# Hybrid decoder layer on one core: the FFN's up projection from seven block products for 768 tokens, the down projection as a stage behind it, the output projection by token groups

## The chip, the core and the metric

The kernel runs on one core of a Trainium2 chip. The metric is the device time of one execution in microseconds (us). The core has five engines with one instruction stream each, and each works through its stream in order: TensorE (PE in the profile) multiplies matrices into PSUM, VectorE (DVE), ScalarE (ACT) and GpSimd (POOL) do elementwise work, and SyncE (SP) issues most of the DMAs. Engines wait for one another by semaphores.

## The reference

One layer is computed for a prompt of 1024 tokens and for 8 samples of 8 tokens, with the same weights, all in fp32 (model width 1024, FFN width 3072). The parts that the change touches are the last three lines of the layer:

```python
m = (g[:, :, 0] * (br_lru @ w_br_lru) + g[:, :, 1] * (br_attn @ w_br_attn)
     + g[:, :, 2] * (br_mem @ w_br_mem))
x = x + rms_norm(m @ w_out, g_post_mix)                       # w_out 1024 x 1024
up, ffn_conv_new = causal_dwconv(rms_norm(x, g_pre_ffn) @ w_up, ffn_conv0, w_ffn_conv, b_ffn_conv)
gate, val = jnp.split(up, 2, axis=-1)                         # w_up 1024 x 6144, convolution of width 3
x = x + rms_norm((jax.nn.gelu(gate) * val) @ w_down, g_post_ffn)   # w_down 3072 x 1024
```

Before them stand a norm, the input projection, a recurrent unit, two kinds of attention and three branch projections. They are the same in both kernels.

## The kernel before, in words

Activations lie with the channel on the partitions and the token along the row: a tensor of width 1024 is 8 tiles of 128 partitions by 1088 elements (1024 prompt tokens, then the 64 sample tokens). The 1088 tokens are worked in three groups, `GROUPS`, of 384, 384 and 320.

Every fp32 operand of a product is split in two: a rounded part (`wh`, `hh`, ...: the cast, on ACT) and the rest (`wl`, `hl`, ...: a subtraction, on POOL for weights, on DVE or POOL for activations). `mm3` issues three matmuls for a pair of tiles: high by high, high by low, low by high. One output tile of 128 channels and one token group of a projection with 1024 inputs is thus 8 x 3 = 24 matmuls into one PSUM bank.

Weights come through `Stream` (L202 to L225): a list of tiles in the order of use. `load` issues the DMA into a raw tile `wr`; `split` issues the cast `wh` (ACT, L209) and the subtraction `wl` (POOL, L211) of 128 x 1024 elements; `get` hands out the next pair; `ahead(raw, sp_)` splits the next `sp_` tiles and loads `raw` more. The split of a tile is issued where `ahead` is called, so it stands in ACT's and POOL's streams behind whatever the program issued before.

Work beside the matmuls is written as generators that hang in two lanes. `pump` advances them a step after each PSUM bank, `drain` runs them to their end. The order of instructions is thus fixed by the program (a scheduler moves single instructions by a few places).

The output projection (L1424 to L1452) goes over the 8 output tiles `j`. For the first three, one weight tile serves all three token groups, 72 matmuls in a row; the other five weight tiles are kept (`kept`) and used group by group, so that `post_mix(g)` (L1388) of one group runs beside the products of the next. `evac_o` copies the bank to `ob` (ACT, L1427) and squares it (ACT, L1353; the squares are added up on DVE, L1357). `unit` calls `W.ahead` behind the evacuation of a tile's first group. `post_mix(g)` needs the sum of squares over the channels (matmuls with a column of ones, L833, whose result `norm_bc` spreads by matmuls, L356), scales `ob` (DVE, L1397), adds the residual (POOL, L1398), does the same sums again for the FFN's norm and splits the result into `h2h` and `h2l`.

The FFN goes in six groups of four tiles (`NFG`, `NG`) of the FFN's width. For each tile `j`, `unit` makes the gate tile and the value tile (a weight tile each, all three token groups, 144 matmuls in all) into the padded tiles `up`, and `ffn_tail` does the convolution of width 3 (`conv`, L596: six DVE instructions of 1024 elements and six of 64 for the two tiles, L600 and L602), the gelu (ACT), the product (DVE, L1506) and the split (ACT, POOL). Behind four tiles the down projection of the group follows and is added to `acc` (DVE, L1691); the last down group is done token group by token group, with the final norm and the outputs behind it. `tail_x` (L1590) fetches the residual for that end.

## Time and profile before

| | |
|---|---|
| median of 3 runs | 2702.36 us (2701.34 to 2702.98) |
| the profiled execution | 2699.19 us, span of its trace 2697.4 us |
| PE busy | 2609.9 us, 97% of the span |
| DVE, ACT, POOL busy | 1248.5 us (46%), 990.3 us (37%), 913.8 us (34%) |
| granted clock of TensorE, mean | 0.986 |
| output projection begins | about 1666 us |
| FFN begins | about 1772 us |
| last group of the down projection begins | about 2610 us |

The span is the time from the first to the last instruction of the trace. The matmul records are pipelined: one is listed with 0.33 us, but the next one starts 0.17 us after it, so durations of PE are read from start to start. "L209" is line 209 of the kernel. The granted clock is the share of full speed (2.4 GHz) that the chip gave TensorE; 0.5 is its lower level, 1.2 GHz.

### The profile page before, as it was taken

What the parts mean: (1) busy time and instruction counts of PE and PEld (TensorE: products, weight loads), DVE (VectorE), ACT (ScalarE), POOL (GpSimd) and SP (SyncE); (2) the same over time, 40 slices, a digit from 0 to 9 for tenths busy, and PEclk for the clock granted to TensorE, in tenths of its full rate; (3) what the DMA queues carried; (4) which work ended last, traced back from release to release, by engine and by line L of the source; (5) the groups of instructions that cost most, each with busy time, mean ns of one, the idle gap of its engine ahead of it and who ended that gap; (6) DMA issues with size and microseconds to landing.
All of it is one profiled execution on the core that took longest, in us unless ns stands there. A gap on an engine that the chain in (4) does not pass through costs nothing.

```text
span 2697.4 us, 43018 instructions
## 1 busy us (share of the span) xinstructions
PE 2609.9 (97%) x16884; PEld 2529.4 (94%) x16884; DVE 1248.5 (46%) x2442; ACT 990.3 (37%) x2071; POOL 913.8 (34%) x939
## 2 busy tenths in 40 slices
PE   8999999998999999999999999999999999999987
PEld 7999999998989898999889999989999999999987
DVE  6465520167686766442333213377052433434357
ACT  6556521254545454445420212343321212222233
POOL 4355422343343433211112122344333343333234
PEclk9999999999999999999999999999999999999998
DMA  9311022221221222324855325141212121111133
GB/s 303 118 40 40 24 66 72 65 78 45 76 69 60 71 68 73 115 85 138 274 183 176 126 88 161 32 150 33 57 40 57 32 60 37 42 48 49 40 108 121
DMA packets 293471, 237.32 MB, mean 88 GB/s; under 512 B 16911, under 2 KB 276792, under 8 KB 293268
## 3 DMA queue, kind: packets, MB, share of 16 engines
q1 hardware_dynamic: 286484, 225.91, 27.0%
q10 hardware_dynamic: 6784, 8.65, 0.9%
q8 instruction: 133, 2.18, 0.3%
q14 instruction: 70, 0.57, 0.1%
HBM read 182.11 MB, written 52.40 MB: 87 GB/s over the span
## 4 chain that ended last, share of the span: by engine, by line
PE 84%; DVE 8%; issue 2%; ACT 2%; POOL 2%; DMA 1%; SPq 0%; ACTq 0%; DVEq 0%; POOLq 0%
PE ps L165 24%; PE ps L167 24%; PE ps L166 24%; PE ps L803 1%; DVE y L927 1%; PE ps L804 1%; PE ps L805 1%; PE ps L908 1%; POOL wl L211 1%; PE ps L910 1%; DVE ob L1397 1%; PE ps L885 1%; PE ps L833 1%; ACT e L933 1%; PE ps L1245 0%
## 5 line engine op out<-in xcount | busy, mean ns | idle before, releaser
L211 POOL TENSOR_TENSOR wl<-wr,wh 128x1024 fp32r<-128x1024 f32 x192 | 472.3, 2464 | 734.3 <-ACT wh L209 517.0
L165 PE MATMUL ps<-hh,wh 128*128 128x384 f32 (+1 forms) x1536 | 513.6, 335 | 2.0 <-ACT e L933 1.0
L167 PE MATMUL ps<-hh,wl 128*128 128x384 f32 (+1 forms) x1536 | 504.0, 328 | 4.2 <-POOL wl L211 4.2
L166 PE MATMUL ps<-hl,wh 128*128 128x384 f32 (+1 forms) x1536 | 503.7, 328 | 0.0
L165 PE MATMUL ps<-h2h,wh 128*128 128x384 f32 (+1 forms) x1152 | 376.6, 328 | 3.2 <-ACT h2h L161 3.2
L166 PE MATMUL ps<-h2l,wh 128*128 128x384 f32 (+1 forms) x1152 | 377.1, 328 | 1.5 <-DVE h2l L162 1.5
L167 PE MATMUL ps<-h2h,wl 128*128 128x384 f32 (+1 forms) x1152 | 376.5, 327 | 0.9 <-POOL wl L211 0.9
L165 PEld LDWEIGHTS ps<-hh,wh 128*128 128x128 f32 x1536 | 290.3, 189 | 14.0 <-issue 7.6
L209 ACT CAST wh<-wr 128x1024 fp32r<-128x1024 f32 x199 | 208.0, 1051 | 253.0 <-PE ps L166 74.3
L167 PEld LDWEIGHTS ps<-hh,wl 128*128 128x128 f32 x1536 | 289.8, 189 | 6.2 <-POOL wl L211 4.8
L166 PEld LDWEIGHTS ps<-hl,wh 128*128 128x128 f32 x1536 | 290.4, 189 | 0.8 <-issue 0.2
L165 PE MATMUL ps<-bh,wh 128*128 128x384 f32 (+1 forms) x768 | 251.2, 328 | 0.0
L166 PE MATMUL ps<-bl,wh 128*128 128x384 f32 (+1 forms) x768 | 250.9, 327 | 0.0
L167 PE MATMUL ps<-bh,wl 128*128 128x384 f32 (+1 forms) x768 | 249.7, 327 | 0.0
L165 PEld LDWEIGHTS ps<-h2h,wh 128*128 128x128 f32 x1152 | 217.1, 189 | 3.5 <-ACT h2h L161 3.5
L166 PEld LDWEIGHTS ps<-h2l,wh 128*128 128x128 f32 x1152 | 217.2, 189 | 2.3 <-DVE h2l L162 2.1
L600 DVE TENSOR_SCALAR cv<-up,pf 128x1024 f32<-128x1024 f32 (+2 forms) x52 | 58.4, 1125 | 346.2 <-ACT up L588 155.5
L167 PEld LDWEIGHTS ps<-h2h,wl 128*128 128x128 f32 x1152 | 217.0, 188 | 1.1 <-POOL wl L211 1.1
L588 ACT COPY up<-ps 128x384 f32<-128x384 f32 (+1 forms) x144 | 63.9, 444 | 364.5 <-PE ps L167 357.5
L166 PE MATMUL ps<-ffl,wh 128*128 128x384 f32 (+1 forms) x576 | 189.6, 330 | 0.0
L167 PE MATMUL ps<-ffh,wl 128*128 128x384 f32 (+1 forms) x576 | 189.0, 332 | 0.2 <-POOL wl L211 0.2
L165 PE MATMUL ps<-ffh,wh 128*128 128x384 f32 (+1 forms) x576 | 187.2, 333 | 1.6 <-DVE acc L1691 1.6
(348 smaller groups left out, 5110.1 us busy)
## 6 DMA issues: line engine op xcount, KB each, us to landing
wr<-in_w_in_dram SPq DMA_DIRECT2D x72, 512.0 KB
wr<-in_w_up_dram SPq DMA_DIRECT2D x48, 512.0 KB
wr<-in_w_down_dram SPq DMA_DIRECT2D x32, 512.0 KB
msd<-sig SPq DMA_DIRECT2D x16, 544.0 KB
brl<-brd SPq DMA_DIRECT2D x16, 544.0 KB
mi<-msd SPq DMA_DIRECT2D x16, 544.0 KB
wr<-in_w_mem_kv_dram SPq DMA_DIRECT2D x16, 512.0 KB
pg<-in_cache_k_dram SPq DMA_DIRECT2D x128, 64.0 KB
```

The source lines that it names most:

```text
L165: pe.matmul(ps, lhsT=lh, rhs=rh, start=start, stop=False)
L166: pe.matmul(ps, lhsT=lh, rhs=rl, start=False, stop=False)
L167: last_mm[0] = pe.matmul(ps, lhsT=ll, rhs=rh, start=False, stop=stop)
L209: (dve.tensor_copy if i == 1 else act.copy)(hi, t)
L211: eng.tensor_tensor(lo, t, f(hi), ALU.subtract)
L588: act.copy(pad[:, hist + g0:hist + g0 + n], ps[:, 0:n])
L600: dve.tensor_scalar(out=o, in0=i, scalar1=wcol(0), scalar2=bcol, op0=ALU.mult, op1=ALU.add)
L803: pe.matmul(o, lhsT=xh, rhs=wh[:, k % 4, :], start=(k == 0), stop=False)
L804: pe.matmul(o, lhsT=xh, rhs=wl[:, k % 4, :], start=False, stop=False)
L805: pe.matmul(o, lhsT=xl, rhs=wh[:, k % 4, :], start=False, stop=(k == NC - 1))
L833: pe.matmul(ps[0:m, i:i + 1], lhsT=sq[:, i * 128:i * 128 + m], rhs=ones[:, 0:1], start=True, stop=True)
L885: pe.transpose(ps[:, i, :], in_=e1[:, (c0 + i) * 128:(c0 + i + 1) * 128], identity=ident)
```

## The change

The output projection now has the token group outside: for each of the three groups all 8 weight tiles are loaded, split and used, 24 units of 24 matmuls each (`W.ahead(1, 1)` stands behind the unit's evacuation and its square). Its inputs lie in tiles `mx_`: for the first two groups they are split where branch 2 ends, for the third by a generator `third_m` that runs beside group 1. In `post_mix` the residual's addition moves from POOL to DVE, and the stores of the new residual are issued in one go. For the last group it splits its result for a plain product; for the first two it forms the operands of the block products: with B11, B12 the upper and B21, B22 the lower half of the 1024 channels for tokens 0 to 383 and 384 to 767, the tiles `T1` to `T4` are sums and differences of them, each split.

The up projection of tile `j` takes [gate; value] as the two block rows (128 channels each) and the two halves of the 1024 inputs as the two block columns: A11, A12, A21, A22. The sums S1 to S4 of the weight blocks are made by four DVE instructions of 128 x 512 (L1735 to L1740), and every operand is cast (ACT) and its rest subtracted (POOL) as a tile `wop` of 128 x 2 x 512. Seven products of 12 matmuls of 384 columns replace eight; the results are put together on DVE out of PSUM (seven additions or subtractions of 384 columns per tile, L1813 to L1836, and one copy on ACT). The last 320 tokens are multiplied as before with A11, A12, A21 and A22 (48 matmuls). For the first two tiles these come behind the block products, from raw weights that are loaded again. The convolution's first step moves from DVE to ACT. The product of gelu and value goes to DRAM (`ff_d`); the down projection follows when all 24 tiles are done, in six groups as before, and reads and splits (`ff_prep`: ACT and DVE) a group of four tiles beside the group before it. `tail_x` is called some groups earlier.

```diff
-RO = (2.0, 1.5)
+RO = (3.0, 3.0)
+OW = (1, 1)
...
-        for j in range(g * NFG, (g + 1) * NFG):
-            for s in range(2):
-                add(("u", j, s), cols(w_up, s * 3 * D + j * 128))
...
+    def conv_steps(pad, sv, hist, out, wcol, bcol):
+        for j in range(hist + 1):
+            for o, i in ((out[:, 0:TP], pad[:, j:j + TP]), (s3(out), sv[:, :, j:j + 8])):
+                if j == 0:
+                    act.activation(out=o, in_=i, func=AF.Identity, scale=wcol(0), bias=bcol)
+                else:
+                    dve.scalar_tensor_tensor(out=o, in0=i, scalar=wcol(j), in1=o, op0=ALU.mult, op1=ALU.add)
+            yield
...
     def post_mix(g):
...
-            pool.tensor_tensor(o, o, x[:, 0:gn], ALU.add)
+            dve.tensor_tensor(o, o, x[:, 0:gn], ALU.add)
...
+            for p in range(4):
+                dve.tensor_tensor(b(0, 0, p), b(0, 1, p), b(0, 0, p), ALU.subtract)
+                t = tmp(384)[:, 0:384]
+                dve.tensor_tensor(t, b(1, 1, p), b(0, 0, p), ALU.subtract)
+                osplit("T2", p, t, pool if p % 2 else dve)
...
-    for j in range(NC - KEPT):
-        out_unit(j, (0, 1, 2), W.get(("o", j)))
-        W.ahead(1, OS[j])
-    kept = {}
-    for g in range(3):
-        for j in range(NC - KEPT, NC):
...
+    def prep_op(i):
...
+        if n == "S2":
+            dve.tensor_tensor(s1, vl[:, lo_], vl[:, hi_], ALU.add)
+            dve.tensor_tensor(s2, s1, gt[:, lo_], ALU.subtract)
+        elif n == "S3":
+            dve.tensor_tensor(gt[:, lo_], gt[:, lo_], vl[:, lo_], ALU.subtract)
+        elif n == "S4":
+            dve.tensor_tensor(gt[:, hi_], gt[:, hi_], s2, ALU.subtract)
...
+        w = slot([128, 2, 4, 128], F32R, "wop")
+        split(src, w[:, 0].rearrange("p k m -> p (k m)"), w[:, 1].rearrange("p k m -> p (k m)"), pool)
...
+    for g in range(3):
+        g0, gn = GROUPS[g]
+        if g == 1:
+            lanes[1].append(third_m())
+        if g == 2:
+            drain((1,))
+        for j in range(NC):
+            wh, wl = W.get(("o", g, j))
+            ps = dense_x(lambda k: wh[:, k, :], lambda k: wl[:, k, :], lambda k: mx_[g][k], gn, NC)
+            act.copy(ob(j, g), ps[:, 0:gn])
+            add_sq(("o", g), ps[:, 0:gn], gn)
+            W.ahead(OW[0], OW[1], O_END)
...
+            pump(*RO)
+        mx_[g] = None
+        lanes[0].append(post_mix(g))
...
+    for i, (j, n) in enumerate(items):
+        if n == "A11g" and j == 0:
+            drain()
...
+        prep_op(i)
+        w = wops.pop(i)
+        if n == "A11":
+            ps = piece(w, op_rhs("B11"), 384, None, True, True)
+            s["p1"] = tmp(384)[:, 0:384]
+            act.copy(s["p1"], ps[:, 0:384])
+        elif n == "A12":
+            ps = piece(w, op_rhs("B21"), 384, None, True, True)
+            dve.tensor_tensor(gates2(s)[0][:, 2:2 + 384], s["p1"], ps[:, 0:384], ALU.add)
+        elif n == "S2":
+            ps = piece(w, op_rhs("T2"), 384, None, True, True)
+            s["u2"] = s.pop("p1")
+            dve.tensor_tensor(s["u2"], s["u2"], ps[:, 0:384], ALU.add)
...
+        prep_op(i + OPA)
...
     for fg in range(NG):
...
+        if fg + 1 < NG:
+            lanes[1].append(ff_prep(fg + 1))
...
-            for g in range(TG, 3):
-                side.append(tail_x(g))
...
+            if fg == NG - 3:
+                for g in range(TG, 3):
+                    side.append(tail_x(g))
```

The stream of ACT in the output projection, before. `ps` is a PSUM bank of one output tile and one token group, `wh` the next weight tile's high part; each line of `ps` belongs to 24 matmuls. Here the second output tile is evacuated, group by group:

```order
L1427 COPY ob2809_17813<-ps2828_17916 128x384
L1353 ACTIVATE t2829_17942<-ps2828_17916 128x384
L209 CAST wh2834_18003<-wr2827_17914 128x1024
L1427 COPY ob2809_17813<-ps2830_17945 128x384
L1353 ACTIVATE t2831_17971<-ps2830_17945 128x384
L209 CAST wh2837_18009<-wr2836_18007 128x1024
L1427 COPY ob2809_17813<-ps2832_17974 128x320
L1353 ACTIVATE t2833_18000<-ps2832_17974 128x320
L1427 COPY ob2810_17814<-ps2840_18015 128x384
L1353 ACTIVATE t2841_18041<-ps2840_18015 128x384
```

And the stream of ACT in the output projection now, in its first token group:

```order
L1760 COPY ob2808_17830<-ps2816_17862 128x384
L1406 ACTIVATE t2817_17888<-ps2816_17862 128x384
L216 CAST wh2818_17890<-wr2800_17751 128x1024
L1760 COPY ob2809_17831<-ps2821_17896 128x384
L1406 ACTIVATE t2822_17922<-ps2821_17896 128x384
L216 CAST wh2823_17925<-wr2820_17894 128x1024
L1760 COPY ob2810_17832<-ps2826_17932 128x384
L1406 ACTIVATE t2827_17958<-ps2826_17932 128x384
L216 CAST wh2828_17961<-wr2825_17929 128x1024
```

Before, the cast of the next weight tile stands behind the first of the three banks that use the present tile, with two banks more to come. Now a tile serves one bank, and the cast of the next tile stands behind that bank's copy and square.

The stream of POOL in the up projection, before. `wl` is a weight tile's rest, `ffl` the rest of an FFN tile; `sp`, `fo` and `up` are small pieces of the convolution's state:

```order
L211 TENSOR_TENSOR wl_19480<-wr_19361,wh_19479 128x1024
L1499 COPY fo_19365<-up_19323 128x2
L1500 COPY fo_19365<-sp_19324 128x16
L162 TENSOR_TENSOR ffl_19496<-cv_19485,ffh_19495 128x1088
L1540 MEMSET up_19552 128x2
L1540 MEMSET up_19556 128x2
L211 TENSOR_TENSOR wl_19587<-wr_19363,wh_19586 128x1024
L1499 COPY fo_19365<-up_19327 128x2
L1500 COPY fo_19365<-sp_19328 128x16
L162 TENSOR_TENSOR ffl_19639<-cv_19628,ffh_19638 128x1088
L211 TENSOR_TENSOR wl_19696<-wr_19483,wh_19695 128x1024
L1499 COPY fo_19365<-up_19552 128x2
```

And the stream of POOL in the up projection now, a little over one tile `j`:

```order
L169 TENSOR_TENSOR wop_21823<-wr_21570,wop_21823 128x512
L169 TENSOR_TENSOR wop_21828<-ws_21739,wop_21828 128x512
L1582 MEMSET up_21880 128x2
L1565 COPY fo_21952<-up_21775 128x2
L1566 COPY fo_21952<-sp_21776 128x16
L169 TENSOR_TENSOR wop_21862<-wr_21572,wop_21862 128x512
L169 TENSOR_TENSOR wop_21887<-wr_21570,wop_21887 128x512
L169 TENSOR_TENSOR wop_21905<-wr_21802,wop_21905 128x512
L169 TENSOR_TENSOR wop_21942<-wr_21802,wop_21942 128x512
L1565 COPY fo_21952<-up_21880 128x2
L1566 COPY fo_21952<-sp_21881 128x16
L1582 MEMSET up_22007 128x2
```

Where two subtractions of 1024 elements for the weights and one of 1088 for the result stood per tile, there are eight of 512 for the weight operands; the result's subtraction has gone from this stream (it is DVE's, in the down stage).

## Rows read from the trace of the kernel before

**Rows 1.** Page, section 4: engines' shares of the chain that ended last.
```profile
PE 84%; DVE 8%; issue 2%; ACT 2%; POOL 2%; DMA 1%; SPq 0%; ACTq 0%; DVEq 0%; POOLq 0%
```

**Rows 2.** Busy by stage: stretch, length, PE, PEld, DVE, ACT, POOL, clock, DMA share, GB/s.
```profile
1666.00:1772.00 106.00, 100.19 (x602) 99.56 (x600) 41.62 (x62) 37.65 (x75) 39.58 (x25) 0.97 0.23 63
1772.00:1847.00 75.00, 69.41 (x394) 66.53 (x394) 51.85 (x83) 32.60 (x66) 34.65 (x44) 0.93 0.43 136
1847.00:2610.00 763.00, 762.80 (x4659) 759.80 (x4659) 293.57 (x408) 191.68 (x328) 271.13 (x259) 1.00 0.15 45
2610.00:2697.00 87.00, 65.38 (x401) 62.91 (x399) 61.62 (x90) 31.64 (x56) 37.17 (x23) 0.86 0.44 152
```

**Rows 3.** Timeline of PE, 320 columns: start us, us, instruction.
```profile
1638.67 0.31 PE L167 MATMUL ps<-bh,wl 128*128 128x320 f32 x1
...
1641.75 0.31 PE L167 MATMUL ps<-bh,wl 128*128 128x320 f32 x1
```

**Rows 4.** Timeline of PE, 384 columns, full clock.
```profile
1643.83 0.33 PE L167 MATMUL ps<-bh,wl 128*128 128x384 f32 x1
...
1646.95 0.33 PE L167 MATMUL ps<-bh,wl 128*128 128x384 f32 x1
```

**Rows 5.** Timeline of a hand-off from PE to ACT.
```profile
1709.60 0.33 PE L167 MATMUL ps<-bh,wl 128*128 128x384 f32 x1
...
1710.03 0.48 ACT L1427 COPY ob<-ps 128x384 f32<-128x384 f32 x1 [3.28 <-PE ps L167]
...
1710.40 0.50 ACT L1353 ACTIVATE t<-ps 128x384 f32<-128x384 f32 x1
```

**Rows 6.** Lines by form, 1560 to 2697 us: busy us, mean ns | idle before, releaser.
```profile
L211 POOL TENSOR_TENSOR wl<-wr,wh 128x1024 fp32r<-128x1024 f32 x96 | 235.7, 2463 | 234.9 <-ACT wh L209 143.7 <-PE ps L166 46.8 <-issue 29.8
...
L602 DVE SCALAR_TENSOR_TENSOR cv<-up,pf,cv 128x1024 f32<-128x1024 f32 x92 | 119.3, 1297 | 0.0
...
L209 ACT CAST wh<-wr 128x1024 fp32r<-128x1024 f32 x95 | 99.2, 1051 | 142.2 <-PE ps L167 62.6 <-PE ps L166 60.0 <-DMA wr<-in_w_down_dram 13.3
...
L1691 DVE TENSOR_TENSOR acc<-acc,ps 128x384 f32<-128x384 f32 x80 | 43.4, 551 | 108.4 <-PE ps L167 108.4
...
L602 DVE SCALAR_TENSOR_TENSOR cv<-sp,pf,cv 128x64 f32<-128x64 f32 x96 | 33.4, 349 | 0.0
L1357 DVE TENSOR_TENSOR t<-t,t 128x384 f32<-128x384 f32 x42 | 32.4, 778 | 48.0 <-ACT t L1353 47.0
L1506 DVE TENSOR_TENSOR cv<-cv,cv 128x1088 f32<-128x1088 f32 x23 | 29.7, 1293 | 4.0 <-ACT cv L1503 2.1
...
L1397 DVE SCALAR_TENSOR_TENSOR ob<-ob,pv,t 128x384 f32<-128x384 f32 x16 | 16.3, 1085 | 4.3 <-ACT t L1367 4.3
...
L162 POOL TENSOR_TENSOR ffl<-cv,ffh 128x384 fp32r<-128x384 f32 x1 | 1.1, 1137 | 0.5 <-ACT ffh L161 0.5
```

**Rows 7.** PE waits by releaser, 1666 to 1772 us: total us, times, longest.
```profile
PE ps L833 <- DVE t L1357: 4.4, 1, 4.4
```

**Rows 8.** Two 10 us windows behind two waits; columns as in rows 2.
```profile
1750.00:1760.00 10.00, 8.55 (x50) 8.50 (x50) 5.86 (x13) 3.19 (x7) 2.15 (x2) 0.74 0.12 35
1780.00:1790.00 10.00, 10.00 (x39) 9.66 (x39) 4.09 (x11) 4.99 (x8) 8.13 (x12) 0.54 0.57 168
```

**Rows 9.** Timeline of DVE and POOL in the FFN stage.
```profile
1957.33 0.84 DVE L600 TENSOR_SCALAR cv<-up,pf 128x1024 f32<-128x1024 f32 x1 [10.73 <-issue]
...
1957.42 0.20 POOL L1500 COPY fo<-sp 128x16 f32<-128x16 f32 x1
...
1962.69 1.21 POOL L1541 COPY sp<-fs 128x16 f32<-128x16 f32 x1 [5.07 <-DVE cv L602]
...
1969.27 2.39 POOL L211 TENSOR_TENSOR wl<-wr,wh 128x1024 fp32r<-128x1024 f32 x1
1969.34 2.93 DVE L600 TENSOR_SCALAR cv<-up,pf 128x1024 f32<-128x1024 f32 x1 [3.98 <-POOL ffl L162]
```

**Rows 10.** PE waits by releaser, 2610 to 2697 us.
```profile
PE ps L1584 <- DMA xl<-x2d: 7.2, 1, 7.2
```

More of the change, by code (lines that the diff above doesn't have):

```diff
@@ L219, in get, with ahead @@
             return self.hl.pop(i)
-        def ahead(self, raw=2, sp_=1):
-            for j in range(sp_):
+        def ahead(self, raw=2, sp_=1, end=None):
+            n = raw + sp_ if end is None else max(0, min(raw + sp_, end - self.i))
+            for j in range(min(sp_, n)):
                 self.split(self.i + j)
-            for j in range(sp_, sp_ + raw):
+            for j in range(sp_, n):
                 self.load(self.i + j)
@@ L1330, in layer_step, with split_m @@
     KEEP = 5
+    G0, G1, G2 = (slice(g0, g0 + gn) for g0, gn in GROUPS)
+    mx_ = [[None] * NC for _ in range(3)]
+    def split_m(j, s):
+        for g in range(2):
+            x = slot((128, T), F32R, "mx")
+            mx_[g][j] = (x[:, G0], x[:, G1])
+            g0, gn = GROUPS[g]
+            split(s[:, g0:g0 + gn], *mx_[g][j])
     def final_m(j, s):
@@ L1340, in final_m, with third_m, ob @@
                 t = slot(name="ml")
-                load(t, ms2[i])
-                mh[i], ml[i] = split_tile(t)
+                load(t[:, 0:768], ms2[i][:, 0:768])
+                split_m(i, t)
+    def third_m():
+        parts = []
+        for i in range(6):
+            x = slot((128, T), F32R, "m2")
+            parts += [x[:, 320 * q:320 * q + 320] for q in range(3)]
+            while len(parts) >= 2 and parts:
+                j = next(j for j in range(NC + 1) if j == NC or mx_[2][j] is None)
+                if j == NC:
+                    break
+                t = tmp(320)
+                load(t[:, 0:320], ms2[j][:, G2])
+                mx_[2][j] = (parts.pop(0), parts.pop(0))
+                yield False
+                split(t[:, 0:320], *mx_[2][j], pool)
+                yield False
     branch(2, load_br(1), RH, final_m)
     x2_d = [dpool.tile([128, T], F32, name=f"x2d{c}") for c in range(NC)]
-    ob = [slot(name="ob") for _ in range(NC)]
+    ob01 = [slot(name="ob") for _ in range(NC)]
+    ob2 = []
+    def ob(j, g):
+        if g < 2:
+            return ob01[j][:, GROUPS[g][0]:GROUPS[g][0] + GROUPS[g][1]]
+        if not ob2:
+            for _ in range(3):
+                x = slot(name="ob2")
+                ob2.extend(x[:, 320 * q:320 * q + 320] for q in range(3))
+        return ob2[j]
     ssq = {}
@@ L1357, in add_sq, with norm_bc @@
             dve.tensor_tensor(ssq[key][:, 0:gn], ssq[key][:, 0:gn], sq[:, 0:gn], ALU.add)
-    def norm_bc(key, gn):
-        for _ in range(dict(x=NYX, f=NYF).get(key[0], NY1)):
+    def norm_bc(key, gn, first=None):
+        for i in range(dict(x=NYX, f=NYF, o=NYO).get(key[0], NY1)):
             yield False
+            if i == 0 and first:
+                first()
         rr = rstd_of(subln_sums(ssq.pop(key), gn), gn, D)
@@ L1416, in post_mix @@
-        for j in range(NC):
-            if g < 2 and j >= HOLD:
-                held[g].append(lambda j=j: h2(j))
-                continue
-            h2(j)
+            o = ob(j, g)
+            h = o
+            dve.scalar_tensor_tensor(out=h, in0=o, scalar=P("g_pre_ffn", j), in1=rb2[:, 0:gn],
+                                     op0=ALU.mult, op1=ALU.mult)
+            p = j % 4
+            if g == 2:
+                hi = opslot("B21" if j >= 4 else "B11", p)[:, G2]
+                lo = opslot("T2" if j >= 4 else "T1", p)[:, G2]
+                h2x[j] = (hi, lo)
+                split(h, hi, lo)
+            elif g == 0:
+                osplit("B21" if j >= 4 else "B11", p, h)
@@ L1450, in layer_step, with dense_x @@
+    def dense_x(wh, wl, xs, gn, nk, ps=None, first=True, last=True):
+        ps = ps or bank()
+        for k in range(nk):
+            mm3(ps[:, 0:gn], wh(k), wl(k), *xs(k), first and k == 0, last and k == nk - 1)
+        return ps
     sfc = a["state_ffn_conv"].rearrange("o b j d -> (o b j) d")
@@ L1461, in load_fs, with put_fo @@
+    def put_fo(j, fo):
+        ft = tmp(256)
+        ps = bank()
         for s in range(2):
[L1462 removed]
+            pe.transpose(ps[0:18, s * 128:(s + 1) * 128], in_=fo[:, s, :], identity=ident)
+        act.copy(ft[0:18, 0:256], ps[0:18, 0:256])
         def put():
[L1465 to L1468 removed]
@@ new lines, in layer_step, with piece, op_rhs, rhs @@
+    blk = {}
+    def piece(w, rhs, gn, ps, first, last):
+        return dense_x(lambda k: w[:, 0, k, :], lambda k: w[:, 1, k, :], rhs, gn, 4, ps, first, last)
+    def op_rhs(name):
+        def rhs(k):
+            x = opt[name, k]
+            return x[:, G0], x[:, G1]
+        return rhs
+    def g2_rhs(half):
+        return lambda k: h2x[4 * half + k]
+    for j in range(NP1):
+        fsput.pop(j)()
+    def gates2(s):
+        s["pg"] = s.get("pg") or pads_of(s["j"], 0)
+        return s["pg"]
```

325 lines of the change are left out of this document (196 added, 129 removed).

## The prediction, made before the changed kernel was run

> **What bounds the kernel now.** I read the chain of waits first: 84% of it is PE, no other engine has more than 8% [rows 1]. A change is worth what it takes from PE, unless something else becomes late. Then busy time by stage, since an average hides the stages the change touches [rows 2]. The reader is to see three things in these rows. In the FFN's long stretch PE is busy 762.80 of 763 us at full clock: there every matmul counts, and DVE (293.57) and POOL (271.13) have room, 74% together. In the output projection PE is idle for 5.8 of 106 us, in the first 75 us of the FFN for 5.6, with the clock at 0.97 and 0.93. In the last down group it is idle for 21.6 of 87.
>
> **The matmuls that go.** A 384-column matmul takes 18 steps in 3.12 us, 0.1733 us each [rows 4]; a 320-column one 21 steps in 3.08 us, 0.1467 [rows 3]. Per FFN tile the first 768 tokens need 7 x 12 = 84 matmuls instead of 96; the last 320 tokens keep 48. So 24 x 12 = 288 matmuls go: 288 x 0.1733 = **-50 us**. Nothing else of PE's work changes in size.
>
> **The output projection, first token group.** The change puts the cast of the next weight tile behind the copy and the square of the present bank on ACT, and only one bank of 24 matmuls uses a tile. That makes a ring. From the start of a bank's last matmul to the copy 0.43 us, to the square 0.37 more [rows 5]; to the cast as much again as between copy and square (0.37, my estimate from the same rows), then the cast 1.05 and POOL's subtraction 2.46 [rows 6]. The third matmul of the next bank needs that result; 21 more follow it, 3.64 us. One turn is 0.43 + 0.37 + 0.37 + 1.05 + 2.46 + 3.64 = 8.3 us for 24 x 0.1733 = 4.16 us of matmuls. Nothing stands in the lanes there yet, so no work covers it: 7 x 4.1 = **+29 us**. Before, two more banks (some 7.7 us) ran behind the cast, which hid all of it. The raw weights are not late: SyncE has little in line there and the DMA share of the stage is 0.23 [rows 2].
>
> **Groups two and three.** The same ring runs with `post_mix` in it. Its steps stand on ACT ahead of casts, and its column sums (six matmuls that wait for DVE) stand on PE between banks. In the order I find five places where PE must wait for more than the ring: three casts behind a run of squares, and two sums that wait for the whole DVE chain of a group. That chain has grown by the additions taken from POOL: 8 scalings at 1.09 us, 8 additions and 7 sums at about 0.78 each [rows 6] are 20 us. These durations were taken beside POOL's subtractions, so that is its long form. It is queued in front of the next bank's sum of squares, and PE's next sum waits for that. The trace of before has this wait once, 4.4 us [rows 7], with two thirds of the chain. Against four banks of 4.16 us that run meanwhile, a chain of 20 us is late by 3 us at least, and by 12 where the additions start late. Nearest to the row of 4.4 is the low end, but there the additions were POOL's; I take 8.4 us for each of the five, **+42 us** (30 to 60).
>
> **The junction.** The old excess goes: 106 us for 384 x 0.1733 + 192 x 0.1467 = 94.7 us of matmuls, 11.3; then 5.6 idle and 7% of 69.4 us of clock, 4.9, together 10.5 [rows 2]. Call it **-22**. In its place come the start of the block products, whose weights stand in POOL's queue behind the subtractions for the operands, some 8 us, and the gates of the first two tiles, which need all of `post_mix` of the third group (16 us by the chain above, with 320 columns, less the block products in front). I take **+23 us** (12 to 30). The two cancel.
>
> **The up stage.** PE needs 84 x 0.1733 + 48 x 0.1467 = 21.6 us per tile, before 23.7. What is new is the load on DVE and POOL. DVE and POOL exclude one another on some instructions [rows 9]: a DVE TENSOR_SCALAR of 1024 elements takes 0.84 us with POOL at rest and 2.93 us when POOL's 2.39 us subtraction has begun 0.07 us before it; a POOL copy of 16 elements takes 0.20 us at 1957 and 1.21 us at 1962, while DVE is in its convolution. So instructions with two SBUF inputs on DVE and all of POOL's add up. Per tile: DVE 4 x 1.30 + 4 x 0.35 + 1.29 for the convolution and the product, and 4 x 0.64 for the weight sums (0.64 for 512 elements is my estimate from 1.29 for 1088 [rows 6]), 10.4 us. POOL 8 subtractions of 512 at 1.40 (between 1.14 at 384 and 2.46 at 1024 [rows 6]), 11.2 us, and six small pieces at 0.2, 1.2 us. Together 22.8 us, over PE's 21.6. DVE has seven more additions out of PSUM, 0.55 each [rows 6], 3.9 us, whose source is not SBUF; if they too find POOL shut out or stand between POOL's work, the sum is 26.7. So a tile costs PE's time and 0.3 us (part of the durations above already holds some waiting) to 5.1 us more. I take 2.0, as a sum of 22.8 leaves no room for two in-order queues that also wait for PE: 22 tiles x 2.0 = **+44 us** (7 to 112). ACT takes the convolution's first step and is far from full: 191.68 of 763 us in the old stage [rows 2].
>
> **The clock.** Behind the 4.4 us wait the next 10 us have a granted clock of 0.74, behind another wait of the junction 0.54 [rows 8]: 2.2 us (26% of 8.55) to 4.6 us lost, at the lower level of 1.2 GHz for part of the time. Before there are three such waits. Now PE waits for about 4 us seven times in the first group, and some seven times for longer. If each cost 2.2 us it would be 31; short waits may cost nothing. I take **+25 us** (0 to 50).
>
> **The rest.** The residual for the end is fetched earlier, so the 7.2 us wait for it [rows 10] goes with some clock behind it: **-10**, and what is late next there is the norm, which is as before. The down stage has its 24 weight splits and additions unchanged; `ff_prep` adds 4 casts and 4 DVE subtractions per 46 us of matmuls. The 24 results pass through DRAM, 0.56 MB each way, in a stage with a DMA share of 0.15 [rows 2], hidden by the matmuls. The first of the six groups has to wait for the last tile's tail: **+5** (0 to 8). Stores of the residual in `post_mix` now go in one piece through SyncE's queue ahead of weight loads; 8 stores of 0.2 MB are covered by the bank in work, and if not it is in the 60 above.
>
> **Sum.** -50 + 29 + 42 - 22 + 23 + 44 + 25 - 10 + 5 = +86 us on the profiled execution of 2699.2 us, 2785. The median is 3.2 us above that execution, so 2788 us.
>
> **Rivals.**
> Output projection late, up stage bound by PE. For it: DVE and POOL are never full in the old stage, and the additions out of PSUM need no port. Against it: 22.8 is more than 21.6 without them. With 7 for the up stage, 35 for groups two and three and 15 for the clock: -50 + 29 + 35 - 22 + 23 + 7 + 15 - 10 + 5 = +32, 2735 us.
>
> Every burst starts slow. If the clock falls in each wait of the output projection, each of 23 banks runs at the lower level from its third matmul on: 21 x 0.1733 = 3.64 us more, 84 us instead of 25, 2847 us. For it: 0.54 in rows 8. Against it: 0.74 in the same rows, and waits of about 4 us as in rows 7. The Trainium skill, "TensorE: Matmul & The Clock Gate", section "HAM oscillation — how this bites in real kernels", tells of a kernel whose short bursts of matmuls between waits each start at the lower clock, and speaks against a loop of this form; by that rule the sum would be this rival's. No run here has a row of such bursts yet. The same time comes if DVE and POOL work fully one after the other: 22 x 5.1 = 112 instead of 44, 2856 us.
>
> Not slower. The ring does not close: casts and subtractions come in time for groups two and three, because `post_mix` in between gives ACT and POOL time to run ahead. Then those groups keep 12 us of waits, the junction 12, the clock loses nothing, the up stage 7: -50 + 29 + 12 - 22 + 12 + 7 - 10 = -22, 2680 us. It decides if the waits outside the first group stay under 34 us together. Against it: the cast stands behind the bank's evacuation in all three groups.
>
> That the change does not do what it says is no rival: PE's listed instructions have the 288 matmuls less, and nothing makes up for them there.
>
> **How the numbers follow.** Forecast 0.52 (2750 to 2825), output projection only 0.21, slow bursts or ports in full 0.15, not slower 0.12. A difference under 0.2% (5.4 us) can't be told from no change; of the last case's 0.12 a quarter falls there. So faster 0.09, same 0.03, slower 0.88. The range leaves out the fast case and the upper end of the slow one: 2708 to 2862 us.
>
> **What the profile after will show.** In the first group of the output projection, PE in bursts of 24 matmuls every 8 us with waits for `wl` of about 4 us; the stage with 60 to 95 us more than before. In the up stage, PE waits for `wop` from POOL, tiles of 23 to 25 us, with DVE and POOL together near 100%. The clock in the output projection near 0.8. The last down group without the wait of 7.2 us. I am wrong if a unit of the output projection takes under 5 us, or if the up stage runs at 21.9 us per tile with PE never waiting; then the second or the last case holds.

## The result, and the profile after

The changed kernel takes 2761.39 us (median of 4 runs, 2760.86 to 2765.28), the kernel before 2702.67 us in the same series: +58.7 us, ratio 1.0219, interval 1.0202 to 1.0237. It is slower, as forecast, inside the range and 27 us under the predicted time. Its profiled execution took 2765.28 us, 66.1 us more than that of before. Of these, 5.2 us lie ahead of the output projection, where the two kernels are nearly the same (it begins at 1665.6 us before and at 1670.8 us now). I count them as scatter between executions: in the runs below, which have the changed kernel's code there, it begins between 1665.3 and 1671.3 us. 61 us are the change's.

The chain of waits has moved away from PE, five points against [rows 1]:

```profile
PE 79%; DVE 7%; issue 5%; POOL 3%; ACT 3%; DMA 2%; SPq 0%; ACTq 0%; DVEq 0%; POOLq 0%
```

Busy time by stage of the changed kernel, in the columns of [rows 2]: first token group of the output projection, the other two, the start of the up stage, the up stage, the down stage, the end.

```profile
1671.00:1750.00 79.00, 51.65 (x193) 46.26 (x193) 5.82 (x11) 14.88 (x25) 16.73 (x8) 0.76 0.31 87
1750.00:1883.00 133.00, 84.80 (x428) 80.70 (x428) 65.56 (x113) 51.01 (x101) 64.58 (x37) 0.76 0.35 102
1883.00:1960.00 77.00, 60.26 (x345) 57.11 (x343) 57.37 (x81) 33.16 (x69) 53.03 (x52) 0.89 0.35 103
1960.00:2426.00 466.00, 466.00 (x2843) 458.16 (x2841) 370.85 (x425) 218.12 (x424) 303.03 (x336) 1.00 0.24 75
2426.00:2704.00 278.00, 278.00 (x1699) 277.71 (x1698) 114.09 (x164) 80.90 (x119) 72.89 (x36) 1.00 0.35 117
2704.00:2763.00 59.00, 43.93 (x266) 41.52 (x264) 42.84 (x75) 16.86 (x30) 25.04 (x18) 0.86 0.37 126
```

The reader should see two halves. In the up and the down stage, 744 us, PE is never idle and the clock is 1.00. Ahead of that, in 289 us, PE is idle for 92 us and runs at 0.76 to 0.89; the same stretch of before had 11 us of idle time in 181 [rows 2]. Who is waited for there:

```profile
PE ps L848 <- DVE t L1410: 31.4, 3, 14.1
PE ps L174 <- POOL wl L218: 26.8, 13, 5.9
PE ps L172 <- ACT wh L216: 24.8, 12, 4.1
...
PE ps L174 <- POOL wop L169: 1.4, 2, 1.0
```

The first row is the column sums that wait for DVE, the next two are the weights of the output projection. The weights of the up stage (`wop`), from which I had expected 44 us, are the last row shown, 1.4 us.

To split the 61 us I take each stage's time from its first matmul to the next stage's first, less 0.1733 us for each of its 384-column and 0.1467 for each of its 320-column matmuls. What is left is waits, lower clock, small matmuls and steps of PE that are a little longer than these:

| us beyond the matmuls | before | now |
|---|---|---|
| output projection, token groups 1 / 2 / 3 | 12.2 together | 45.5 / 33.5 / 37.8 |
| start of the FFN | 15.8 | 24.7 |
| steady FFN; now up 15.0 and down 6.5 | 11.1 | 21.5 |
| last down group | 35.9 | 22.8 |
| sum | 75.0 | 185.8 |

185.8 - 75.0 - 49.9 (the 288 matmuls) = +60.9 us.

One turn of the first token group, in a timeline of the changed kernel: the last matmul of a unit, copy, square and cast on ACT, the next unit's first matmul, the subtraction on POOL, and the first matmul that needs it.

```profile
1706.31 0.34 PE L174 MATMUL ps<-mx,wl 128*128 128x384 f32 x1
1706.69 0.48 ACT L1760 COPY ob<-ps 128x384 f32<-128x384 f32 x1 [8.18 <-PE ps L174]
1707.06 0.50 ACT L1406 ACTIVATE t<-ps 128x384 f32<-128x384 f32 x1
1707.44 1.05 ACT L216 CAST wh<-wr 128x1024 fp32r<-128x1024 f32 x1
...
1708.54 0.52 PE L172 MATMUL ps<-mx,wh 128*128 128x384 f32 x1 [1.89 <-ACT wh L216]
1708.57 2.35 POOL L218 TENSOR_TENSOR wl<-wr,wh 128x1024 fp32r<-128x1024 f32 x1 [7.64 <-ACT wh L216]
...
1710.97 0.69 PE L174 MATMUL ps<-mx,wl 128*128 128x384 f32 x1 [1.58 <-POOL wl L218]
```

From 1706.31 to 1710.97 are 4.66 us. The prediction's sum for this piece was 0.43 + 0.37 + 0.37 + 1.05 + 2.46 = 4.68. The rest of the turn is longer than forecast: the seven turns take 10.35 us on average ((1749.6 - 1677.1) / 7), not 8.3, and the matmul at 1710.97 is listed with 0.69 us where [rows 4] has 0.33.

### The profile page after: what moved, and what is told of

Same layout as the page of the kernel before. It is cut to its first block, busy times and chain, and to the rows that moved or that the text cites. A ratio compares the mean times of both kernels' runs of the same rounds, so it can differ in the third digit from the quotient of the medians.

```text
span 2763.3 us, 43739 instructions
## 1 busy us (share of the span) xinstructions
PE 2599.4 (94%) x16596; PEld 2504.4 (91%) x16596; DVE 1461.9 (53%) x2677; ACT 1113.3 (40%) x2323; POOL 1065.6 (39%) x1074
## 4 chain that ended last, share of the span: by engine, by line
PE 79%; DVE 7%; issue 5%; POOL 3%; ACT 3%; DMA 2%; SPq 0%; ACTq 0%; DVEq 0%; POOLq 0%
PE ps L172 23%; PE ps L174 23%; PE ps L173 22%; POOL wl L218 2%; DVE y L942 1%; PE ps L818 1%; PE ps L819 1%; PE ps L820 1%; PE ps L923 1%; PE ps L900 1%; PE ps L925 1%; ACT e L948 1%; DVE e L956 1%; POOL wop L169 0%; PE ps L1260 0%
## 5 line engine op out<-in xcount | busy, mean ns | idle before, releaser
L218 POOL TENSOR_TENSOR wl<-wr,wh 128x1024 fp32r<-128x1024 f32 x160 | 391.0, 2447 | 878.5 <-ACT wh L216 672.1
L172 PE MATMUL ps<-bop,wop 128*128 128x384 f32 (+1 forms) x1056 | 349.1, 331 | 1.6 <-ACT bop L168 1.6
L173 PE MATMUL ps<-bop,wop 128*128 128x384 f32 (+1 forms) x1056 | 345.0, 327 | 2.2 <-DVE bop L169 2.2
L174 PE MATMUL ps<-bop,wop 128*128 128x384 f32 (+1 forms) x1056 | 344.6, 327 | 2.2 <-POOL wop L169 1.4
L172 PEld LDWEIGHTS ps<-hh,wh 128*128 128x128 f32 x1536 | 290.0, 189 | 14.2 <-issue 7.6
L169 POOL TENSOR_TENSOR wop<-wr,wop 128x512 fp32r<-128x512 f32 x150 | 242.3, 1630 | 36.0 <-ACT wop L168 35.0
L216 ACT CAST wh<-wr 128x1024 fp32r<-128x1024 f32 x167 | 173.7, 1049 | 131.0 <-DMA msd<-sig 68.4
L744 DVE TENSOR_TENSOR sig<-sig,ps 128x384 f32<-128x384 f32 (+1 forms) x72 | 38.3, 531 | 312.0 <-PE ps L174 312.0
L174 PEld LDWEIGHTS ps<-bop,wop 128*128 128x128 f32 x1056 | 199.0, 188 | 3.3 <-POOL wop L169 1.9
L172 PEld LDWEIGHTS ps<-bop,wop 128*128 128x128 f32 x1056 | 199.1, 189 | 2.8 <-ACT bop L168 1.8
L173 PEld LDWEIGHTS ps<-bop,wop 128*128 128x128 f32 x1056 | 199.1, 189 | 2.6 <-DVE bop L169 2.6
L172 PE MATMUL ps<-bh,wh 128*128 128x384 f32 (+1 forms) x576 | 188.6, 327 | 0.0
L173 PE MATMUL ps<-bl,wh 128*128 128x384 f32 (+1 forms) x576 | 188.3, 327 | 0.0
L174 PE MATMUL ps<-bh,wl 128*128 128x384 f32 (+1 forms) x576 | 188.1, 327 | 0.0
```

Source lines behind the costliest of these rows:

```text
L169: (on_lo or dve).tensor_tensor(lo, src, f(hi), ALU.subtract)
L172: pe.matmul(ps, lhsT=lh, rhs=rh, start=start, stop=False)
L173: pe.matmul(ps, lhsT=lh, rhs=rl, start=False, stop=False)
L174: last_mm[0] = pe.matmul(ps, lhsT=ll, rhs=rh, start=False, stop=stop)
L216: (dve.tensor_copy if i == 1 else act.copy)(hi, t)
L218: eng.tensor_tensor(lo, t, f(hi), ALU.subtract)
```

## Experiments

**The cast ahead of the matmuls.** In the output projection's loop:

```diff
             wh, wl = W.get(("o", g, j))
+            W.ahead(OW[0], OW[1], O_END)
             ps = dense_x(...)
             act.copy(ob(j, g), ps[:, 0:gn])
             add_sq(("o", g), ps[:, 0:gn], gn)
-            W.ahead(OW[0], OW[1], O_END)
```

> Changed kernel, with one edit: in the output projection the next weight tile's cast and subtraction are issued ahead of the present unit's matmuls, not behind its evacuation. Ring theory (the wait is the serial chain copy, square, cast, subtraction): the 7 turns of the first token group fall from 10.35 us to about 4.2 us each, -43 us, and the weight waits of groups two and three (some 27 us) mostly go, the DVE waits at the column sums (32 us) stay: about 2695 us. Rival, the raw weight loads or POOL's queue are late too: each unit then takes as long as a load or the 2.5 us subtraction with its hand-offs allows, 6 to 8 us, and the time falls by 20 to 30 us only: about 2735 us.

Measured: 2713.82 us, 47.6 under the changed kernel (ratio to before 1.0041, 1.0027 to 1.0055). By stage (first group; second and third), and PE's waits up to the steady up stage:

```profile
1669.00:1706.00 37.00, 35.02 (x198) 33.71 (x197) 7.17 (x10) 13.52 (x23) 19.14 (x8) 1.00 0.64 180
1706.00:1829.50 123.50, 80.13 (x425) 76.27 (x425) 64.96 (x111) 50.31 (x99) 61.45 (x36) 0.77 0.38 112
```

```profile
PE ps L848 <- DVE t L1410: 30.4, 3, 13.0
PE ps L174 <- POOL wl L218: 13.8, 5, 5.8
PE ps L172 <- ACT wh L216: 7.6, 3, 3.4
```

The ring is open: the first group takes 36.3 us, not 78.8, 3.1 beyond its matmuls, at full clock, and raw loads don't hold it. But the other half of the expectation failed: groups two and three keep 62.0 of their 71.3 us. The sums still wait 30 us, and eight waits for weights stay, 21.4 us together. One tile of lead was enough in the first group and not in the two where `post_mix` shares ACT and POOL.

**Filler in the ring.** In seven units of the first group, matmuls whose result is not used, where PE waits:

```diff
+            if g == 0 and j:
+                last_fill = filler(last_mm[0])            # 12 matmuls of 384 columns ahead of the unit
...
+                    second = pe.matmul(ps[:, 0:gn], lhsT=wh[:, k, :], rhs=rl, start=False, stop=False)
+                    if k == 0:
+                        last_fill = filler(second)        # 12 more ahead of the first with wl
```

> Changed kernel, with 24 matmuls of 384 columns added in each of the last seven units of the first token group, whose result nobody uses: 12 stand where PE waits for the high part of the weights, 12 where it waits for the low part, 2.1 us each in gaps of 2.2 us. Clock theory: of the 10.35 us of a turn, 8.3 are the chain and 2.05 the lower clock behind the waits; with PE kept busy the clock stays up and a turn takes 8.3 us: about -14 us, 2747 us, with a granted clock near 1.0 in that stretch. Rival, the turn is long for another reason (a longer hand-off, late loads): no gain, 2761 us, or up to +7 us where the filler delays the unit.

Measured: 2751.20 us, 10.2 less. The first group, in the changed kernel and here:

```profile
1671.00:1739.00 68.00, 44.99 (x168) 40.23 (x167) 5.08 (x10) 12.11 (x21) 14.08 (x6) 0.75 0.32 90
```

```profile
1671.00:1733.00 62.00, 61.25 (x347) 59.22 (x345) 3.35 (x6) 13.37 (x23) 16.75 (x7) 1.00 0.39 109
```

PE does 168 matmuls more and the stretch ends earlier: it is busy for 61.25 of 62 us and the clock is 1.00 where it was 0.75. The whole group takes 65.7 us, not 78.8, and a turn 8.5 us (five turns from 1681.09 to 1723.51), where the prediction's sum was 8.3. So some 1.9 us of each turn of 10.35 were the lower clock. It is a diagnosis and no remedy, since the waits stay.

**More work for POOL in the up stage.** Two of the eight subtractions per tile are done twice:

```diff
+        if j >= NP1 and n in ("A11", "S1"):
+            pool.tensor_tensor(w[:, 1]..., src, f(w[:, 0]...), ALU.subtract)
```

> Changed kernel, with two of the eight POOL subtractions of 512 elements per FFN tile done twice for 22 tiles (POOL +2.6 us per tile). Shared-port theory: DVE's instructions with two SBUF inputs and POOL's work add up to some 21 of the 21.85 us of a tile already (the union of both in the trace is 96%), so 2.6 us more make a tile 1.0 to 1.8 us longer: +20 to +40 us, 2781 to 2801 us, with PE waiting for the weight operands. Rival, each engine has its own room (POOL at 62 to 72%): no change, 2761 us.

Measured: 2772.64 us, +11.2, between the two. The up stage itself grew by 5.4 us (451.1 us of matmuls at 21.6 are 20.9 tiles), its start by 4.5. A stretch of 300 us in the changed kernel and here:

```profile
2100.00:2400.00 300.00, 300.00 (x1830) 294.65 (x1830) 229.12 (x269) 139.60 (x271) 185.75 (x215) 1.00 0.24 76
```

```profile
2100.00:2400.00 300.00, 300.00 (x1829) 294.93 (x1828) 242.80 (x271) 140.07 (x265) 232.98 (x242) 1.00 0.23 74
```

POOL is busy 47 us more and PE still for 300 of 300, with the same number of matmuls. Nearly all of the growth is at the start: the first four tiles with double work take 25.6, 23.5, 24.5 and 24.1 us, and from the sixth on a tile takes 22.3 to 22.4 us as in the changed kernel. Here are the first 51 us; the changed kernel has 314 matmuls there and no idle time:

```profile
1949.00:2000.00 51.00, 47.93 (x286) 45.67 (x285) 42.80 (x43) 21.87 (x41) 39.80 (x40) 1.00 0.24 65
```

So in the settled stage two more subtractions cost nothing. The union of both engines' busy times, from which I had read a full path, includes their waiting for each other, so it says nothing about room.

Then all eight, with the same line and without its condition on `n`:

> Changed kernel, with all eight POOL subtractions of 512 elements per FFN tile done twice for 22 tiles (POOL +10.3 us per tile, to some 21.5 of its own 21.85). Two more per tile cost the up stage only 5 us, so an instruction can't hold the other engine out for all of its time. Short-hold theory: each holds the shared way for its elements only (some 1.1 of POOL's 1.29 us, 1.1 of DVE's 1.27, 0.07 of its 0.27): 16.8 us per tile in the changed kernel, 19.0 with two more, 25.5 here, so a tile takes 3 to 4.5 us longer: +65 to +100 us, about 2840 us. Rival, no exclusion that counts: POOL is just full by itself, 0 to +20 us, 2761 to 2781 us.

Measured: 2903.99 us, +142.6, more than either theory: the up stage takes 123.6 us more, 5.9 per tile, and a settled tile 28.4 us where it took 22.3. The same stretch, and what PE waits for in it:

```profile
2100.00:2400.00 300.00, 252.30 (x1429) 241.28 (x1429) 227.08 (x209) 106.76 (x209) 275.08 (x254) 0.95 0.18 58
```

```profile
PE ps L172 <- ACT wop L168: 42.9, 19, 4.7
```

PE is busy for 252 of 300 us. It waits for ACT's casts, and ACT in turn stands idle for 56.6 us behind DVE's convolution before it casts the weight sums. The rival falls: POOL's sixteen subtractions at about 1.3 us and its small pieces would fit a tile, but their means here are 1.36 to 1.74 us (one of four rows is shown), and DVE is stretched too. DVE's lines, changed kernel first, then this one with a row of POOL:

```profile
L616 DVE SCALAR_TENSOR_TENSOR cv<-up,pf,cv 128x1024 f32<-128x1024 f32 x53 | 67.6, 1276 | 25.7 <-ACT cv L614 25.7
...
L1826 DVE TENSOR_TENSOR up<-t,ps 128x384 f32<-128x384 f32 x14 | 7.8, 555 | 21.4 <-PE ps L174 21.4
```

```profile
L616 DVE SCALAR_TENSOR_TENSOR cv<-up,pf,cv 128x1024 f32<-128x1024 f32 x42 | 73.2, 1760 | 0.0
...
L1829 DVE TENSOR_TENSOR up<-t,ps 128x384 f32<-128x384 f32 x11 | 6.1, 555 | 17.0 <-PE ps L174 17.0
...
L169 POOL TENSOR_TENSOR wop<-wr,wop 128x512 fp32r<-128x512 f32 x65 | 109.3, 1687 | 0.0
```

The step with two operands in SBUF goes from 1.28 to 1.76 us, the addition out of PSUM stays at 0.555. The Trainium skill, "GPSIMD Engine Reference", section "Key points", has GpSimd share its SBUF interfaces with VectorE, with contention for DVE's instructions with two SBUF inputs; the two rows of each DVE pair agree.

How full was the path in the changed kernel? For three forms the trace gives the shortest, median and longest ns in that stretch:

```profile
L616 DVE SCALAR_TENSOR_TENSOR cv<-up,pf,cv x53: 1270/1273/1287, 2105.8 to 2396.0; 128x1024 f32<-128x1024 f32 x53
L616 DVE SCALAR_TENSOR_TENSOR cv<-sp,pf,cv x53: 270/1315/1337, 2108.7 to 2398.9; 128x64 f32<-128x64 f32 x53
...
L169 POOL TENSOR_TENSOR wop<-wr,wop x81: 1276/1302/2249, 2099.0 to 2398.4; 128x512 fp32r<-128x512 f32 x81
```

The second row shows how much of a duration can be waiting: the step of 64 elements takes 0.27 us at its shortest and 1.3 us in the median. At their shortest, DVE's instructions with two SBUF inputs need 4 x 1.27 + 4 x 0.27 + 1.29 [rows 6] + 4 x 0.68 (the weight sums) = 10.2 us per tile, POOL 8 x 1.28 and some 1.4 for its small pieces, 11.6: together 21.8 us, 24.3 with two more subtractions, 32.0 with eight. The settled tiles took 22.3, 22.3 and 28.4 us. So these times don't all lie one behind the other: some 2 us overlap with two more, at least 3.6 with eight. That is an estimate from three kernels. The edge lies between two and eight more subtractions per tile.

**The residual's addition back on POOL.**

```diff
-            dve.tensor_tensor(o, o, x[:, 0:gn], ALU.add)
+            pool.tensor_tensor(o, o, x[:, 0:gn], ALU.add)
```

> Changed kernel, with the residual's addition behind the output projection put back on POOL as in the kernel before. If the length of DVE's chain is what PE's column sums wait for (32 us in four waits), taking 8 x 0.55 us from DVE per group shortens each wait by 3 to 4 us: -8 to -12 us, about 2751 us. Rival, the square and sum behind each addition then wait for POOL, whose addition takes 1.3 us and stands behind the 2.5 us weight subtractions: no gain or longer, 2761 to 2780 us.

Measured: 2766.02 us, +4.6: the rival, by little. PE's waits:

```profile
PE ps L174 <- POOL wl L218: 29.8, 14, 5.8
PE ps L848 <- DVE t L1410: 27.5, 3, 11.6
```

The sums wait 4 us less (27.5), the weights' rests 3 us more (29.8). Moving the addition to DVE was not what made the change slow.

**Where sums and casts stand.** Three variants of the kernel with the cast first. Two tiles split ahead of use:

```diff
-OW = (1, 1)
+OW = (1, 2)
```

> Changed kernel with the cast ahead of the matmuls (the kernel of 2713.8 us), and the split one tile further ahead: two tiles are split ahead of use, not one. Theory, the weight waits left in groups two and three (3.4 + 5.5 us and 3.7 + 6.3 us, with smaller ones some 22 us) come from casts and subtractions that stand behind the norm's work on ACT and POOL: one unit more of lead takes most of them away, -10 to -20 us, 2694 to 2704 us. Rival, the waits for DVE's chain at the column sums (10.2 and 13.3 us) only grow by what is saved ahead of them: 0 to -8 us, about 2710 us.

Measured: 2705.67 us, -8.1 (ratio 1.0015, 1.0005 to 1.0024), at the border of the two. Then the sums later, with one tile ahead as in the first experiment:

```diff
-NYX = 3
+NYX = 11
-RO = (3.0, 3.0)
+RO = (4.0, 3.0)
```

> The kernel of 2713.8 us, with the steps beside the matmuls taken four per unit, not three, and eight more empty steps ahead of the second column sum of each group, so that DVE's chain starts some 0.7 unit earlier and PE meets the sum about 1.1 units later. Theory, the waits of 10.2 and 13.3 us at the sums come from where the sum stands in PE's stream: they shrink by 5 to 7 us each, with some clock behind them -12 to -20 us, 2694 to 2702 us. Rival, what follows the sum (operands of the block products) is then late by as much: no gain, 2710 to 2720 us.

Measured: 2713.52 us, no gain: the rival. Its waits:

```profile
PE ps L848 <- DVE t L1410: 14.2, 2, 7.7
...
PE ps L174 <- POOL wl L218: 9.3, 6, 3.8
```

The sums' waits halve, from 30.4 to 14.2, and others take their place: the third group has 16.1 us beyond its matmuls where it had 32.2, the start of the up stage 42.4 where it had 26.3. From the end of the second group to the steady up stage it is 139.6 us without the edit and 139.7 with it. Third, one FFN tile more whose 320-token part comes late:

```diff
-NP1 = 2
+NP1 = 3
```

> The kernel of 2713.8 us, with three FFN tiles, not two, whose 320-token part is put behind their block products (14.6 us more of matmuls ahead of the wait for the third group's norm). Theory, the junction's 16 us of waits (7.8 at the column sum, 2.2, 1.3, 2.0, 2.7 around it) are DVE's chain of the third group: they go but for the hand-offs, -8 to -14 us, about 2702 us. Rival, DVE and POOL are shared with the operands and the weights of the block products, so the chain is late by as much again: 0 to -4 us, about 2711 us.

Measured: 2716.14 us, +2.3: the rival, and a little worse. The wait at the third group's sum is 8.8 us, before 7.5.

**Both edits, and the chain made shorter.** The two edits to `OW` and to `NYX` and `RO` together:

> The two edits to the out-projection loop joined: split two tiles ahead (2705.7 us) and the sums later in PE's stream with four steps per unit (2713.5 us). Chain theory: from the last product of the second token group to the steady up stage the time was 138 to 140 us in every variant, wherever single waits stood, because the block products need the finished norm of both groups and its operands, and only 28.5 us of other matmuls lie beside that; so no gain over the first of the two, 2702 to 2710 us. Rival, the waits are a matter of where sums and casts stand: each edit takes its own, 2690 to 2697 us.

Measured: 2705.00 us (ratio 1.0009, 1.0000 to 1.0019), -0.7 against the first of them alone, which is no gain: the kernel before itself moved by 1.5 us between the two series. So far it is the chain theory. The second token group became 8.8 us shorter, and the stretch from its end to the steady up stage 8.6 us longer. And the chain itself, in the kernel with two tiles ahead, leaving out the residual:

```diff
-            dve.tensor_tensor(o, o, x[:, 0:gn], ALU.add)
```

> The kernel of 2705.7 us, leaving out the residual's addition ahead of the FFN's norm (8 DVE additions per token group; the FFN then sees the normed projection alone). Chain theory: each group's chain of DVE work, ACT squares and sums is 8 x 0.55 us shorter, and PE waits for the end of it in each group: -9 to -14 us, 2692 to 2697 us. Rival, the additions are hidden beside the squares or the waits come from the weights' casts: 0 to -3 us, 2703 to 2706 us.

Measured: 2694.76 us (ratio 0.9966, 0.9953 to 0.9978), -10.9. PE's waits with the residual, and then without:

```profile
PE ps L848 <- DVE t L1410: 33.2, 4, 14.6
PE ps L174 <- POOL wop L169: 11.2, 4, 8.6
PE ps L174 <- POOL wl L218: 6.7, 3, 5.0
```

```profile
PE ps L848 <- DVE t L1410: 18.8, 4, 8.1
PE ps L174 <- POOL wop L169: 11.1, 4, 8.9
PE ps L174 <- POOL wl L218: 7.1, 3, 5.3
```

The waits at the sums fall by 14.4 us, of the others only one changes by much (that for `wop` from ACT, 0.5 to 4.4). So the length of `post_mix`'s chain counts in PE's time here. One limit: with the addition goes also DVE's wait for the residual's load, which the timeline of the changed kernel shows inside that chain. Here is the end of the first group's chain in it:

```profile
1770.55 1.48 DVE L1463 TENSOR_TENSOR ob<-ob,t 128x384 f32<-128x384 f32 x3
...
1771.39 0.34 PE L174 MATMUL ps<-mx,wl 128*128 128x384 f32 x1
...
1774.10 1.03 DVE L1463 TENSOR_TENSOR ob<-ob,t 128x384 f32<-128x384 f32 x2 [0.67 <-DMA t<-xsd]
...
1775.96 0.56 DVE L1463 TENSOR_TENSOR ob<-ob,t 128x384 f32<-128x384 f32 x1 [0.82 <-DMA t<-xsd]
...
1776.44 2.15 DVE L1410 TENSOR_TENSOR t<-t,t 128x384 f32<-128x384 f32 x4
...
1778.50 1.68 DVE L1463 TENSOR_TENSOR ob<-ob,t 128x384 f32<-128x384 f32 x2
...
1780.31 1.69 DVE L1410 TENSOR_TENSOR t<-t,t 128x384 f32<-128x384 f32 x3
...
1781.58 1.44 PE L848 MATMUL ps<-ones,t 128*128 128x1 f32 x6 [9.85 <-DVE t L1410]
```

DVE's additions stop twice behind a load, at 1774.10 and at 1775.96; PE has begun its last matmul of a unit at 1771.39 and stands until the sum at 1781.58. In the kernel with two tiles ahead DVE stands idle for such loads for 1.6 us in all. But no run takes the loads away alone, so how the 10.9 us divide between the additions and the loads stays open.

**Other work ahead.** The kernel with two tiles ahead, with the products of the first token group first and four weight operands ahead:

```diff
-OPA = 2
+OPA = 4
-    items = [(j, n) for j in range(NP1) for n in SEVEN] + \
+    items = [(j, n) for j in range(NP1) for n in SEVEN[:2]] + \
+        [(j, n) for j in range(NP1) for n in SEVEN[2:]] + \
```

> The kernel of 2705.7 us, with the four products that need only operands of the first token group (A11 and A12 of the first two FFN tiles) ahead of all others, and their four weight operands made before the up stage begins (four ahead, not two). Chain theory: 4.2 us more of matmuls lie beside the operands' chain, and the weight operands no longer stand behind it on ACT and POOL (a wait of 9 us at the first product): -5 to -12 us, 2694 to 2701 us. Rival, the norm of the third group, whose sum the first gates wait for, comes later by what is put ahead of it on POOL and ACT: 0 to +5 us, 2705 to 2711 us.

Measured: 2704.78 us, -0.9, at the rival's edge: the wait of 8.6 us for `wop` falls to 2.8, and the third group's sum waits 8.4 us where it waited 7.5. Last, all order edits in one (`NYX = 9` here):

> All order edits in one: cast ahead of the matmuls, two tiles ahead, four steps per unit with six more empty steps ahead of the second sum, four products of the first group's operands first with four weight operands ahead. Chain theory: the chain of post_mix on DVE, ACT and POOL sets the time from the end of the first token group to the steady up stage (210 us in the changed kernel, 194 to 203 in its variants), so the join gives 0 to -5 us over the best single one: 2699 to 2706 us, the same as the kernel before. Rival, the edits add up as their single waits do: 2690 to 2697 us, faster than the kernel before.

Measured: 2698.78 us in 11 runs (ratio to before 0.9986, 0.9977 to 0.9995), -6.0 against the best single variant. It lies 0.2 us below the chain theory's range and 1.8 us above its rival's. The time is 0.14% under the kernel before, less than the 0.2% which the prediction called no difference. From the end of the first group to the steady up stage it takes 186.7 us, the changed kernel 210.4, the one with the cast first about 203, the one without the residual 185.9. So order alone took as much from this stretch as order and a shorter chain did. PE's waits in it:

```profile
PE ps L848 <- DVE t L1410: 16.6, 4, 6.7
...
PE ps L362 <- POOL y L860: 8.5, 5, 3.8
```

The sums wait 16.6 us, with the four products ahead but the sums not later it was 33.9. Against the join of two edits (2705.0) the gain lies at the start of the up stage, 97.1 us there and 87.9 here: presumably the products that were put ahead fill time beside the chain only when the sums stand later. Each of the two edits, added alone to the kernel with two tiles ahead, had gained under 1 us.

## Why the prediction was right, and where it was not

- **The matmuls that go, -50:** right. The up stage runs at full clock with PE never idle, with 288 matmuls less.
- **The output projection, first group, +29:** the wait is right to the piece, 4.66 against 4.68 us, and shown by the edit that opens the ring: 42 of the 47.6 us came from this group (45.5 to 3.1). 13 of the 45.5 are the clock's, by the filler (78.8 to 65.7); without them it is 32.5 for 29.
- **Groups two and three, +42:** right in place and, nearly, in size. PE is idle for 48.2 of the 133 us, inside the range of 30 to 60, and waits for sums behind DVE and for casts and rests of weights, as forecast; the whole excess, clock included, is 71.3. I had named the waits as separate places; the runs show that they hang together. One sum moved brought its wait back elsewhere (139.6 and 139.7 us), a shorter chain gained 10.9 us, and all order edits together took 15.0 from the kernel with the cast first. The block products need the finished norm and the operands of 768 tokens before most of them can start, while before the first FFN tiles went group by group. That this dependence is the reason is argued from the order of the program; no run tests it alone.
- **The junction, -22 and +23:** the old excess was 28.0, the new 24.7 with its clock, so the two nearly cancel, as forecast.
- **The up stage, +44:** this is the step that failed. "A sum of 22.8 leaves no room for two in-order queues": the sum was a little too high (21.8 at the shortest times, with 1.28 and not 1.40 us for a POOL subtraction), and even 24.3 fitted, since some of it overlaps. The forecast of `wop` waits did not come true: no PE wait was listed in the up stage, and a settled tile takes 22.3 us with PE never idle, close to the 21.9 that the prediction had named as a sign against itself. Up and down stage together cost 10.4 us more than the old steady stretch (21.5 and 11.1). That is PE's own work: in the up stage matmuls of 384 columns follow one another after 0.176 us on average (0.174 in the old stage), not 0.1733, and small matmuls come between. The exclusion is real, as the doubled POOL work shows, but its edge lay more than two subtractions per tile away. The term's lower end, 7 us, came near the measured size, but was meant for waits.
- **The clock, +25:** about +32. (1 - 0.76) x 51.65, 0.24 x 84.80 and 0.11 x 60.26 make 39.4 us; before it was 3.0 and 4.9. By the rival in which every bank runs slow it would be 84. In the first group the seven turns took 9.9 to 10.9 us each at a granted clock of 0.83 to 0.68, and 8.5 us with the filler at 1.00: some 1.9 us lost per turn, where a bank wholly at the lower level loses 3.64. The Trainium skill, "TensorE: Matmul & The Clock Gate", section "HAM oscillation — how this bites in real kernels", tells of bursts between waits that each start at the lower clock. The trace agrees in that the clock was lowered in every one of the seven turns; the price here is about half of a burst wholly at the lower level.
- **The rest:** the wait of 7.2 us [rows 10] is gone, and the end has 22.8 us beyond its matmuls instead of 35.9, -13 for -10. What PE waits for there now:

```profile
PE ps L1604 <- POOL acc L1598: 1.8, 4, 0.7
PE ps L362 <- POOL y L860: 1.8, 1, 1.8
```

Up to down cost nothing that a wait shows. The rival "output projection late, up stage bound by PE", 2735 us, named the right places; its time was short mainly because groups two and three and the clock cost more. Term by term, the output projection has 116.8 us beyond its matmuls where the forecast had 96 with the clock (29 + 42 + 25), and the up and down stages 10.4 more than before where it had 49 (44 + 5); the junction and the end are within 5 us. So the forecast came as close as it did by two errors of opposite sign, 39 us that did not come and 21 that came in addition. That part is luck.

## What to carry to other kernels

When a loop turns so that a weight tile serves fewer matmuls, walk once round the ring: from the last matmul through evacuation, cast and rest to the first matmul that needs them, against the matmuls that one tile feeds. If it doesn't fit, move the cast ahead of the work, and a tile further ahead where other work shares its engine. A wait behind a long chain on another engine can come back elsewhere when one sum or one cast is moved: here single moves gained between -2 and 8 us, all of them together 15. So judge such an edit by the time from the chain's start to its last user, not by the wait that it moves; shorten the chain, or put more independent work beside it. Durations of two engines that share a path hold their waiting for each other, and their sum can't show that the path is full: take the shortest times, or double one side and see.

## What the runs showed of the hardware

Useless matmuls in a wait made the kernel 10.2 us faster, by holding the granted clock at 1.00 instead of 0.75. DVE and POOL hold one another up (a DVE step of 0.27 us takes 1.3 in the median), but this cost PE time only past an edge: two more POOL subtractions of 512 elements per tile cost a settled tile nothing (22.3 us), eight cost it 6.1 us (28.4).
